# A mixture-of-experts forward pass: weights read in 32 KB runs per partition, with the contraction axes permuted to match

## The chip, the cores and the metric

The kernel runs on one NeuronCore of a Trainium2 chip. Five engines work side by side: TensorE (PE in the profile, its weight loads shown apart as PEld), VectorE (DVE), ScalarE (ACT), GpSimd (POOL) and SyncE (SP). Sixteen DMA engines move data between HBM and the on-chip SBUF; matmul results land in PSUM. The metric is the time of one execution in microseconds (us), lower is better.

## The reference

Eight experts, each with 256 tokens of width 512 and two weight matrices, all float32 in HBM:

```python
def reference(x, w1, w2):          # x (8,256,512)  w1 (8,512,2048)  w2 (8,2048,512)
    h = np.matmul(x, w1)
    h = np.maximum(h, 0)
    return np.matmul(h, w2).astype(np.float32)
```

One expert reads 4.19 MB of `w1`, 4.19 MB of `w2` and 0.52 MB of `x`, and writes 0.52 MB. No weight is used twice.

## The kernel before

All eight experts go through one loop. The DMA queue of GpSimd casts: it reads float32 weights and writes bf16 into SBUF, so 4.19 MB read become 2.10 MB written. `x` comes in as float32 through SP's queue.

**Layouts.** For a matmul, the axis that is summed over must lie on the 128 partitions. Before, partition `p` holds row `ko*128 + p` of a weight matrix for every block `ko`: four separate rows of `w1` (8 KB each in HBM) and sixteen separate rows of `w2` (2 KB each). The same holds for `x` and the output, with two rows of 2 KB per partition.

**One expert.** `x_sbuf` is transposed in eight 128x128 blocks in float32 (L65); each block goes to one PSUM tile and is copied, cast to bf16, by ScalarE (L68) before the next one may use that tile. The first layer (L79) is 64 matmuls: a 128x128 block of `w1` is the stationary operand and 256 columns of the transposed `x` stream past it. ScalarE applies the ReLU to pairs of results (L87). The second layer (L113) is 32 matmuls: a block of `hT` is stationary and 512 columns of `w2` stream. The loop over the two halves `mo` of the tokens is outside, the loop over the sixteen blocks `ko` inside. VectorE copies each half out of PSUM (L120) and SP stores both at once (L122).

**What sets the order.** Each engine runs its instructions in a fixed order that a scheduler wrote at build time; between engines there are semaphores. GpSimd issues the weight loads in the order w1, w2, w1, w2 (L71, L102), one queue, first in first out on each DMA engine. Both weight pools have four buffers, so the loads of four experts are queued at once and the load for expert e+4 is issued when expert e has been multiplied. The last expert's `w2` comes in four pieces of four blocks. The scheduler puts the last five transposes of an expert between its first matmuls of the first layer.

## Time and profile before

| what | value |
|---|---|
| median of three timed runs (lowest, highest) | 196.74 us (196.43, 199.07) |
| span of the profiled execution, first to last instruction | 196.1 us |
| its own time around the span | not listed; median minus span is 0.6 us |
| PE busy | 142.4 us, 73% |
| ACT busy, DVE busy, POOL busy | 55.4, 11.1, 17.8 us |
| weight queue (q0) as a share of 16 DMA engines | 93.7% |

The page's busy shares are averages over the whole span. For this kernel the DMA row of the 40 slices is the one to look at first: it reads 9 (90% or more) in all but the first and the last three slices, while the PE row changes between 5 and 9. "GB/s" counts what lands: for weights that is bf16, so the read side is twice that; `x` and the output count at their float32 size.

### The profile page before, as it was taken

Reading aid. Unit: us, or ns where it says so; the run is one execution under the profiler, and the core shown is the slowest. Engines: PE = TensorE matmul, PEld = TensorE weight load, DVE = VectorE, ACT = ScalarE, POOL = GpSimd, SP = SyncE. Lnnn points to the kernel's source line nnn. Section 1 sums busy time; section 2 is a strip of 40 time slices with the busy share of each in tenths; the row PEclk is TensorE's granted clock in tenths of the full one; section 3 lists DMA queues with packets and bytes.
Section 4 is the critical chain, followed back from the end, with each engine's and each line's share of the span. In section 5 each row is a group of like instructions: output and inputs, shape, how many; then the busy total and the mean of one; then the engine's idle time right before and its main releaser. Section 6 shows DMA issues by size and latency. Waiting matters only on the chain.

```text
span 196.1 us, 1934 instructions
## 1 busy us (share of the span) xinstructions
PE 142.4 (73%) x832; PEld 86.1 (44%) x832; DVE 11.1 (6%) x16; ACT 55.4 (28%) x129; POOL 17.8 (9%) x25
## 2 busy tenths in 40 slices
PE   0102899869398785959489696958997695959990
PEld 0001485348133572337334374425853482437740
DVE  0000000200011000200001100110002000200011
ACT  2100262137101470026300363022721271024500
POOL 8900001200102000020100100010001000010000
PEclk9999999999979999999958999995899999996999
DMA  5999999999999999999999999999999999999702
GB/s 206 226 236 203 200 232 242 208 243 252 225 216 205 250 255 218 214 221 249 244 216 208 208 259 253 216 206 253 212 218 208 248 212 219 215 216 237 121 0 107
DMA packets 25143, 42.05 MB, mean 214 GB/s; under 512 B 560, under 2 KB 16944, under 8 KB 25136
## 3 DMA queue, kind: packets, MB, share of 16 engines
q0 software_dynamic: 20784, 33.56, 93.7%
q1 hardware_dynamic: 4352, 8.39, 12.6%
q8 instruction: 6, 0.10, 0.2%
q14 instruction: 1, 0.01, 0.0%
HBM read 71.30 MB, written 4.19 MB: 385 GB/s over the span
## 4 chain that ended last, share of the span: by engine, by line
PE 58%; DMA 25%; another core or an unknown queue 7%; ACT 4%; POOL 2%; issue 2%; DVE 0%; POOLq 0%; ACTq 0%
PE o_psum L113 27%; DMA w_c<-in_w_dram 25%; PE h_psum L79 24%; PE xpsum L65 7%; ACT xT_sbuf L68 4%; POOL w_sbuf L71 1%; POOL w_c L102 1%; DVE out_sbuf L120 0%; POOL identity masks.py:199 0%; POOL identity masks.py:197 0%; POOLq masks.py:199 0%; ACTq L68 0%; POOLq L137 0%
## 5 line engine op out<-in xcount | busy, mean ns | idle before, releaser
L79 PE MATMUL h_psum<-xT_sbuf,w_sbuf 128*128 128x256 bf16 x512 | 67.3, 288 | 20.0 <-DMA w_sbuf<-in_w_dram 17.1
L113 PE MATMUL o_psum<-w_c,hT_sbuf 128*128 128x512 bf16 x256 | 61.3, 401 | 13.4 <-DMA w_c<-in_w_dram 13.4
L79 PEld LDWEIGHTS <-w_sbuf 128*128 128x128 bf16 x512 | 53.8, 106 | 30.5 <-DMA w_sbuf<-in_w_dram 18.4
L68 ACT CAST xT_sbuf<-xpsum 128x128 bf16<-128x128 f32 x64 | 17.0, 266 | 111.0 <-PE xpsum L65 111.0
L113 PEld LDWEIGHTS <-hT_sbuf 128*128 128x128 bf16 x256 | 25.9, 103 | 46.5 <-DMA w_c<-in_w_dram 11.1
L87 ACT ACTIVATE hT_sbuf<-h_psum 128x512 bf16<-128x512 f32 x64 | 37.1, 597 | 18.3 <-PE h_psum L79 18.1
L65 PE MATMUL xpsum<-identity,x_sbuf 128*128 128x128 f32 x64 | 22.0, 344 | 15.9 <-ACT xT_sbuf L68 11.3
L65 PEld LDWEIGHTS xpsum<-identity,x_sbuf 128*128 128x128 f32 x64 | 9.8, 153 | 28.0 <-ACT xT_sbuf L68 22.3
L120 DVE COPY out_sbuf<-o_psum 128x512 f32<-128x512 f32 x16 | 11.1, 692 | 181.4 <-PE o_psum L113 181.4
L102 POOL DMA_DIRECT2D w_c<-in_w_dram x11 | 11.2, 1014 | 100.2 <-PE xpsum L65 100.2
L71 POOL DMA_DIRECT2D w_sbuf<-in_w_dram x8 | 6.2, 779 | 53.6 <-PE h_psum L79 53.3
L68 ACT ACT_TABLE_LOAD x1 | 1.3, 1283 | 0.7 <-PEq L137 0.7
masks.py:199 POOL TENSOR_SCALAR_AFFINE_SELECT identity<-identity 128x128 f32<-128x128 f32 x1 | 0.3, 304 | 0.1
masks.py:197 POOL MEMSET identity<- 128x128 f32 x1 | 0.2, 204 | 0.3 <-POOLq L137 0.3
L137 POOL MEMSET const-float32-0.0<- 128x1 f32 x1 | 0.1, 98 | 0.2 <-issue 0.2
L137 POOL MEMSET const-bfloat16-1.0<- 128x1 bf16 x1 | 0.1, 101 | 0.0
L137 POOL MEMSET const-uint8-127<- 128x1 uint8 x1 | 0.1, 101 | 0.0
L137 POOL MEMSET const-float32-1.0<- 128x1 f32 x1 | 0.1, 98 | 0.0
## 6 DMA issues: line engine op xcount, KB each, us to landing
w_sbuf<-in_w_dram POOLq DMA_DIRECT2D x8, 2048.0 KB, 77.7
w_c<-in_w_dram POOLq DMA_DIRECT2D x7, 2048.0 KB, 80.7
x_sbuf<-in_x_dram SPq DMA_DIRECT2D x8, 512.0 KB, 7.7
out_dram<-out_sbuf SPq DMA_DIRECT2D x8, 512.0 KB, 6.9
w_c<-in_w_dram POOLq DMA_DIRECT2D x4, 512.0 KB, 42.1
```

The source lines that it names most:

```text
L65: nc.tensor.transpose(xpsum[:], x_sbuf[:, mo, ko * P:(ko + 1) * P], identity)
L68: nc.scalar.copy(xT_sbuf[:, ko, mo * P:(mo + 1) * P], xpsum[:])
L71: nc.gpsimd.dma_start(w1_sbuf[:], w1_tiled[e])
L79: nc.tensor.matmul(h_psum[:, mo_sub2 * capacity:(mo_sub2 + 1) * capacity], w1_sbuf[:, ko, mo * P:(mo + 1) * P], xT_sbuf[:, ko, :], start=( ...
L87: nc.scalar.activation(hT_sbuf[:, mo:mo + 2, :], h_psum[:], mybir.ActivationFunctionType.Relu,)
L102: nc.gpsimd.dma_start(w2_c[:], w2_tiled[e, :, ch * k2_chunk:(ch + 1) * k2_chunk, :])
L113: nc.tensor.matmul(o_psum[:], hT_sbuf[:, ko, mo * P:(mo + 1) * P], w2_sb[ch][:, ko_sub, :], start=(ko == 0), stop=(ko == K2 - 1),)
L120: nc.vector.tensor_copy(out_sbuf[:, mo, :], o_psum[:])
L137: nc = _bacc.Bacc("TRN2", target_bir_lowering=False, num_devices=1)
```

## The change

Which row of the summed axis lies on which partition is free, as long as both operands agree. The change numbers the rows the other way round: partition `p` takes consecutive rows. For `w1`, rows 4p to 4p+3, which is 32 KB in one piece in HBM; for `w2`, rows 16p to 16p+15, also 32 KB; for `x` and the output, rows 2p and 2p+1, 4 KB. With J = 16, hidden unit n = 16q+j must land on partition q of block j, so the stationary block of `w1` is now taken with a step of 16 columns, 32 bytes in bf16 (`w1_r[:, ko, b, :, j]`). `x` must be split as column 4q+ko: it is cast to bf16 on VectorE (`xb`), transposed in eight blocks with a step of four columns into one PSUM bank, and copied out by one VectorE instruction. The loads are issued one expert ahead of use in the program text, the depth of the weight pools stays four. The last expert's `w2` comes in pieces of 4, 4, 4, 2, 1 and 1 blocks in buffers of their own; its second layer loops over blocks outside and token halves inside, and its two halves are copied by VectorE and ScalarE and stored by SP and by ScalarE's queue.

```diff
-    x_tiled = x.rearrange("e (mo p) k -> e p mo k", p=P)
-    w1_tiled = w1.rearrange("e (ko p) n -> e p ko n", p=P)
-    w2_tiled = w2.rearrange("e (ko p) n -> e p ko n", p=P)
+    x_v = x.rearrange("e (p mo) k -> e p (mo k)", mo=MC)
+    out_v = out.rearrange("e (p mo) k -> e p (mo k)", mo=MC)
+    w1_v = w1.rearrange("e (p ko) n -> e p (ko n)", ko=K1)
+    w2_v = w2.rearrange("e (b p j) n -> e p b (j n)", p=P, j=J)
...
+            pieces = [4, 4, 4, 2, 1, 1]
+                c = w2_pool.tile([P, n * H], BF16, name=f"w2_last{i}", bufs=1)
+                nc.gpsimd.dma_start(c[:], w2_v[e, :, b, j * H:(j + n) * H])
...
-                nc.tensor.transpose(
-                    xpsum[:], x_sbuf[:, mo, ko * P:(ko + 1) * P], identity
-                )
-                nc.scalar.copy(xT_sbuf[:, ko, mo * P:(mo + 1) * P], xpsum[:])
+        nc.vector.tensor_copy(xb[:].rearrange("p m q k -> p (m q k)"), xs[e][:])
+        xt_ps = psum_t.tile([P, K1, MC, P], BF16, name="xt_ps")
+                nc.tensor.transpose(xt_ps[:, ko, mo, :], xb[:, mo, :, ko], identity[:])
+        nc.vector.tensor_copy(
+            xT[:].rearrange("p k c -> p (k c)"),
+            xt_ps[:].rearrange("p k m q -> p (k m q)"),
+        )
...
+        w1_r = w1s[e][:].rearrange("p (ko b q j) -> p ko b q j", ko=K1, b=NB, j=J)
-                        w1_sbuf[:, ko, mo * P:(mo + 1) * P],
+                        w1_r[:, ko, b, :, j],
...
+        if last:
+            order = [(k, m) for k in range(K2) for m in range(MC)]
+        else:
+            order = [(k, m) for m in range(MC) for k in range(K2)]
...
+                if last and m == 1:
+                    nc.scalar.copy(out_sb[:, m, :], o_ps[m][:])
+                else:
+                    nc.vector.tensor_copy(out_sb[:, m, :], o_ps[m][:])
+                if last:
+                    eng = nc.scalar if m == 1 else nc.sync
+                    eng.dma_start(out_v[e, :, m * H:(m + 1) * H], out_sb[:, m, :])
```

**Weight queue, GpSimd, end of the program.** Before (L71 loads `w1`, L102 `w2`; the shapes are partitions x rows x columns):

```order
L71 DMA w_sbuf<-in_w_dram 128x4x2048
L102 DMA w_c<-in_w_dram 128x16x512
L71 DMA w_sbuf<-in_w_dram 128x4x2048
L102 DMA w_c<-in_w_dram 128x4x512 x4
L148 UNCONDITIONAL_BRANCH
```

And of the change, the same place (L64 loads `w1`, L72 `w2`, L82 the last expert's pieces):

```order
L64 DMA w_sb<-in_w_dram 128x8192
L72 DMA w_sb<-in_w_dram 128x8192
L64 DMA w_sb<-in_w_dram 128x8192
L82 DMA w_last_932<-in_w_dram 128x2048
L82 DMA w_last_934<-in_w_dram 128x2048
L82 DMA w_last_936<-in_w_dram 128x2048
L82 DMA w_last_938<-in_w_dram 128x1024
L82 DMA w_last_940<-in_w_dram 128x512
L82 DMA w_last_942<-in_w_dram 128x512
```

The order of the loads is the same; each is now one run per partition, and the last `w2` is cut finer towards its end.

**TensorE, between the second layer of the seventh expert and the first layer of the eighth.** Before, from the transposes (L65) of the eighth expert on:

```order
L65 MATMUL xpsum_1143<-identity_58,x_sbuf_1140 128x128
L65 MATMUL xpsum_1146<-identity_58,x_sbuf_1140 128x128
L65 MATMUL xpsum_1149<-identity_58,x_sbuf_1140 128x128
L79 LDWEIGHTS w1_sbuf_1167
...
L65 MATMUL xpsum_1152<-identity_58,x_sbuf_1140 128x128
L65 MATMUL xpsum_1155<-identity_58,x_sbuf_1140 128x128
```

And of the change, the same place (L105 are the transposes, L119 the first layer, L140 the second):

```order
L140 MATMUL o_ps_1040<-w2_sb_793,hT_957 128x512
L105 LDWEIGHTS xb_1076
L105 MATMUL xt_ps_1078<-identity_88,xb_1076 128x128
...
L119 LDWEIGHTS w1_sb_929
L119 MATMUL h_ps_1090<-xT_1087,w1_sb_929 128x256
```

All eight transposes now stand ahead of the first layer, none between its matmuls.

**TensorE, the end of the last expert's second layer.** Before, where the first token half ends and the second begins (`o_psum_1259` and `o_psum_1277` are the halves, `w2_c_1250` the first piece of `w2`, `w2_c_1256` the last):

```order
L113 MATMUL o_psum_1259<-w2_c_1256,hT_sbuf_1169 128x512
L113 LDWEIGHTS hT_sbuf_1169
L113 MATMUL o_psum_1277<-w2_c_1250,hT_sbuf_1169 128x512
...
L113 MATMUL o_psum_1277<-w2_c_1256,hT_sbuf_1169 128x512
L148 UNCONDITIONAL_BRANCH
```

And of the change, the last rows (`o_ps_1171` and `o_ps_1172` are the halves):

```order
L140 MATMUL o_ps_1172<-w2_last3_938,hT_1089 128x512
L140 LDWEIGHTS hT_1089
L140 MATMUL o_ps_1171<-w2_last4_940,hT_1089 128x512
L140 LDWEIGHTS hT_1089
L140 MATMUL o_ps_1172<-w2_last4_940,hT_1089 128x512
L140 LDWEIGHTS hT_1089
L140 MATMUL o_ps_1171<-w2_last5_942,hT_1089 128x512
L140 LDWEIGHTS hT_1089
L140 MATMUL o_ps_1172<-w2_last5_942,hT_1089 128x512
```

Before, 20 of the 32 matmuls stand behind the first one that needs the last piece; now two matmuls need it, and they are the last ones.

## Rows read from the trace of the kernel before

**Rows 1.** DMA queues of the page: packets, MB landed, share of 16 engines.
```profile
q0 software_dynamic: 20784, 33.56, 93.7%
q1 hardware_dynamic: 4352, 8.39, 12.6%
```

**Rows 2.** Waits: engine, line, for whom; us in total, times, longest.
```profile
PE h_psum L79 <- DMA w_sbuf<-in_w_dram: 17.1, 6, 12.1
PE o_psum L113 <- DMA w_c<-in_w_dram: 13.4, 5, 3.4
```

**Rows 3.** Stretches with only w1 arriving: busy by engine, clock, DMA share, GB/s.
```profile
121.50:128.50 7.00, 7.00 (x33) 3.12 (x33) 0.69 (x1) 0.00 (x0) 0.00 (x0) 1.00 1.07 216
143.50:150.50 7.00, 6.73 (x32) 2.98 (x30) 1.03 (x2) 0.53 (x2) 0.08 (x1) 1.00 1.07 216
164.50:171.50 7.00, 6.86 (x33) 2.98 (x30) 0.90 (x2) 0.05 (x1) 0.00 (x0) 1.00 1.07 216
```

**Rows 4.** Same view, stretches with only w2 arriving.
```profile
108.50:112.50 4.00, 2.62 (x15) 1.32 (x13) 0.69 (x1) 1.55 (x6) 0.74 (x1) 1.00 1.24 208
158.00:162.00 4.00, 4.00 (x39) 3.52 (x36) 0.00 (x0) 3.12 (x6) 0.00 (x0) 1.00 1.24 208
180.00:183.00 3.00, 3.00 (x30) 2.69 (x29) 0.00 (x0) 2.45 (x5) 0.00 (x0) 1.00 1.25 207
```

**Rows 5.** Same view, the first two us, and where the load stream ends.
```profile
0.00:2.00 2.00, 0.00 (x0) 0.00 (x0) 0.00 (x0) 1.26 (x1) 1.14 (x6) 1.00 0.00 0
184.00:185.00 1.00, 1.00 (x10) 0.77 (x8) 0.00 (x0) 0.72 (x2) 0.00 (x0) 1.00 0.51 83
```

**Rows 6.** Timeline, PE and DVE in the tail: start, length, what [idle before].
```profile
164.17 7.08 PE L113 MATMUL o_psum<-w_c,hT_sbuf 128*128 128x512 bf16 x32 [1.98 <-DMA w_c<-in_w_dram]
173.90 0.61 PE L79 MATMUL h_psum<-xT_sbuf,w_sbuf 128*128 128x256 bf16 x4 [1.11 <-DMA w_sbuf<-in_w_dram]
178.24 6.56 PE L79 MATMUL h_psum<-xT_sbuf,w_sbuf 128*128 128x256 bf16 x52 [0.35 <-ACT xT_sbuf L68]
184.63 7.07 PE L113 MATMUL o_psum<-w_c,hT_sbuf 128*128 128x512 bf16 x32
191.74 0.69 DVE L120 COPY out_sbuf<-o_psum 128x512 f32<-128x512 f32 x1 [2.76 <-PE o_psum L113]
```

**Rows 7.** Chain of waits: start, length, what; first layer at full and at half clock.
```profile
156.35 5.84 PE h_psum L79 x52
175.30 0.44 PE h_psum L79 x4
176.82 0.85 PE h_psum L79 x4
```

**Rows 8.** Weight loads and transposes by line: ns min/median/max.
```profile
L79 PEld LDWEIGHTS <-w_sbuf x512: 95/98/208, 18.6 to 184.4; 128*128 128x128 bf16 x171
L113 PEld LDWEIGHTS <-hT_sbuf x256: 95/98/152, 30.5 to 191.1; 128*128 128x128 bf16 x128
L65 PEld LDWEIGHTS xpsum<-identity,x_sbuf x64: 137/138/231, 4.4 to 177.3; 128*128 128x128 f32 x64
L65 PE MATMUL xpsum<-identity,x_sbuf x64: 272/328/476, 4.4 to 177.5; 128*128 128x128 f32 x64
```

**Rows 9.** Timeline of GpSimd at the start: first weight load behind the identity's memset.
```profile
0.74 0.20 POOL masks.py:197 MEMSET identity<- 128x128 f32 x1 [0.29 <-POOLq L137]
1.27 0.87 POOL L71 DMA_DIRECT2D w_sbuf<-in_w_dram  x1 [0.33 <-issue]
```

**Rows 10.** Stretches around a fall of the PE clock (columns as in rows 3).
```profile
98.00:99.00 1.00, 0.39 (x1) 0.13 (x2) 0.00 (x0) 0.00 (x0) 0.00 (x0) 0.50 1.11 223
177.00:178.00 1.00, 0.89 (x5) 0.52 (x3) 0.00 (x0) 0.20 (x2) 0.00 (x0) 0.50 1.13 291
```

**Rows 11.** Timeline, PE: the first matmul in the first stretch of rows 10.
```profile
98.61 0.61 PE L113 MATMUL o_psum<-w_c,hT_sbuf 128*128 128x512 bf16 x1 [3.41 <-DMA w_c<-in_w_dram]
```

## The prediction

> **What bounds the kernel now.** I read the page's DMA queues first [rows 1]. The weight queue's packets fill 93.7% of sixteen engines. Its 20784 packets are 16384 rows of `w2` (2 KB read, 1 KB landed), 4096 rows of `w1` (8 KB read) and 16 for each of 19 loads: one packet for one run in HBM. Then the waits [rows 2]: TensorE waits for weights in both layers, 17.1 and 13.4 us, while the loads of four experts stand queued, so nothing holds the stream back. Then the busy time by stretches. Nothing lands in the first 2.0 us; in the second from 184 on 83 GB/s are left of some 208, so the stream ends at 184.4 [rows 4, 5]. Where only `w1` arrives, 216 GB/s land, 432 read [rows 3]; where only `w2` does, 208, or 416 read [rows 4]. At these rates a matrix (2.097 MB landed) takes 9.71 or 10.08 us, eight of each 158.3 us. Of the 182.4 us of stream 24.1 remain for eight `x` and seven outputs, 1.6 us each. Last the timeline of the tail [rows 6]: the eighth expert's first layer starts at 173.9, its second at 184.6, and the span ends at 196.1, 11.7 us after the stream. So the time is 2.0 of start, 182.4 of stream, 11.7 of tail.

> **The change, part by part.**

> *Longer runs.* One engine takes 2048 bytes at 416/16 = 26.0 GB/s in 78.8 ns, and 8192 at 27.0 in 303.4 ns [rows 3, 4]. The line through both is 3.9 ns a packet plus 27.4 GB/s. By it 32768 bytes take 1202 ns: 436 GB/s read, 218 landed, 9.62 us a matrix. That saves 0.46 us on each `w2`, 0.09 on each `w1`, 4.4 us over eight experts. `x` and the outputs go from 2 to 4 KB: 8 packets fewer per engine and transfer, 0.03 us, times 15 is 0.5 us. I take -4.9. Bounds: if long runs reach only the rate of 8 KB, `w2` alone gains 0.37 x 8 = 3.0; if they change nothing, 0. I take the line, since both of its points are the same queue in the same execution; that 32 KB lies fourfold beyond its last point stays in the range.

> *Start.* The first weight load is issued at 1.27, behind the identity's memset that started at 0.74 [rows 9]; now it stands first. Between 0 and -0.5; I take -0.4, as the queue's own start-up is the same.

> *Tail.* Let T be the end of the stream. Before, `w1` of the last expert was there 10.5 us ahead of T (173.9 to 184.4), 0.4 more than its `w2` alone takes, the share of an output stored meanwhile. Now 9.62 + 0.4: T-10.0. The first layer is 64 pairs of a weight load and a matmul; 52 took 5.84 us at full clock [rows 7], 112 ns each, so 7.2 us, no longer broken up by transposes: T-2.8. The second layer takes 7.08 us [rows 6]. It works through pieces as they land and only two matmuls need the last, so the weights do not hold it: T+4.3. A copy of 0.69 us, then the store: from the copy's end at 192.43 to the span's end 3.67 us [rows 6]. The two halves now go through two queues, but nearly together and with the same bytes, so I keep 3.67 (-0.5 is the other end). End: T+8.6 against T+11.7, -3.1 us.

> *TensorE in the steady state.* Per expert: first layer 7.2, second 7.08, eight transposes at between 0.098 (a hidden bf16 load) and 0.328 us (today's float32 matmul) [rows 8], 0.8 to 2.6, taken as 1.2 since they no longer wait for a copy each; then one copy of 1024 columns, nearest row 0.69 for 512 [rows 6], 0.7 to 1.4, taken as 1.2. Sum 16.7 us. The stream needs 2 x 9.62 + 1.57 for an output = 20.8. So 4.1 us are slack, and all of this costs nothing as long as a pair of the first layer stays under 112 + 4100/64 = 176 ns. If that cover goes, every ns above it costs 64 x 8 ns.

> *The step of 16 columns.* No row has a stationary load with a step. The contiguous ones take 98 ns at full clock and 152 at half [rows 8]: some 53 ns go with the clock, 45 do not, and all of it is hidden under the matmul, as the pair's 112 ns show. Bounds: hidden as now, 112 ns a pair; far end, the part that goes with the clock eightfold, some 430 ns. I take 112; a doubled part (151 ns, wholly exposed) would add 39 x 64 = 2.5 us, in the tail alone.

> [...]

> *Without cost.* VectorE gains eight casts and eight copies, at most 2.8 us per expert beside 1.4 of today, within 20.8. ScalarE loses its copies. SP's queue now holds six loads of `x` ahead of the first output. A packet of `x` then alternates with a weight packet of 1.2 us, eight times per engine, so `x` lands in about 10.8 us; it is issued an expert or more ahead, and the first one delays only the first layer's start, which no term of the sum holds. The last pieces of `w2` have buffers of their own, and wait only for loads that landed long before.

> **Sum.** -4.9 - 0.4 - 3.1 = -8.4 us on the profiled span of 196.1: 187.7. The median of the runs is 0.6 above that span, so **188.3 us**.

> **Rivals.**

> *TensorE becomes the bound (slower).* If the step makes a pair of the first layer take 213 ns, as at half clock (0.85 us for four [rows 7]), an expert needs 13.6 + 7.08 + 2.4 = 23.1 us, more than the stream's 20.8. First layer from about 14 us on, 8 x 20.7, 7 x 2.4 between, 4.4 at the end: 200.8, or 201.4 with the 0.6. It decides from 176 ns; at 430 ns it would be about 312 us. For it: every column lies in another place, and no row bears on that. Against it: the load may grow from 98 to 176 ns unseen. Chance 0.13.

> *Long runs bring nothing.* If both matrices go on at today's rates, or the sixteen engines, now walking runs that lie 128 KB apart, lose as much as the packets save, start and tail alone remain: -3.5, 193.2 us. For it: 2 to 8 KB brought only 4% [rows 3, 4]. Against it: 4% per packet is what is on offer, and `w1`, with the longer run, is the faster of the two. Chance 0.13. Should the queue cut the runs into 8 KB packets, so that the change does not do what it says, `w2` still gains 3.0 us: 190.2, inside the forecast's own range.

> *The clock.* TensorE's clock fell to half after a wait of 3.41 us [rows 10, 11], and again at 177, between waits for copies, costing the last first layer part of its speed. With slack of 4.1 us per expert it can fall again; only the last expert pays, 1.6 us for 3.4 us at half clock, 6.4 for a whole first layer. This is no case of its own but the upper part of the forecast.

> **How the numbers follow.** The forecast, stream still the bound and 186 to 192 us, has 0.74; the two rivals 0.13 each. The measurement tells 2% from no change, that is 192.8 and 200.7 us. So faster 0.74; within 2%, the second rival, 0.13; slower, the first, 0.13. The range takes in the forecast, its unknowns below (a line that runs on better, a quicker store) and the second rival: 185.3 to 196; outside it are the first rival and some 0.05 below.

> **What would show it.** Packets of the weight queue: 15 x 128 runs, 6 x 128 pieces and 21 x 16, or 3024. Landed rate 218 in both kinds of stretch; 208 would mean the second rival. Stream's end near 179. First-layer pairs at 112 ns and TensorE waiting for weights twice per expert; a weight load above 170 ns with TensorE never waiting would be the first rival. Behind the stream, the second layer's end 4.3 and the span's end 8.6 us later. The forecast is wrong if the stream's rate falls, or if TensorE's own 16.7 us become 20.8.

## The result and the profile after

The changed kernel takes **188.66 us** (median of four runs, 188.61 to 188.91) against 197.91 of the kernel before beside it (196.43 to 199.21): a ratio of 0.9545, 95% interval 0.9474 to 0.9617. Forecast were 188.3 us. The span of its profiled execution is 186.9 us, its own time 188.91, so 2.0 us lie around a span. I had put 0.6 there, the median before minus a span from another run; in the runs of the kernel before that stand beside the experiments it is some 1.8. On the spans alone the forecast was 187.7 and 186.9 came out: 9.2 us less instead of 8.4.

The DMA queues of the changed kernel (packets, MB landed, share of sixteen engines) answer to [rows 1]:

```profile
q0 software_dynamic: 3024, 33.56, 84.7%
q1 hardware_dynamic: 2304, 8.13, 11.5%
```

3024 packets, as worked out: every run of 32 KB is one packet. Its waits, which answer to [rows 2]:

```profile
PE h_ps L119 <- DMA w_sb<-in_w_dram: 28.3, 7, 10.6
PE o_ps L140 <- DMA w_sb<-in_w_dram: 17.2, 7, 3.7
```

TensorE still waits for weights in both layers, longer than before; the stream is still the bound. The end of the stream by seconds (busy time by engine, clock, DMA share, GB/s) answers to [rows 5]:

```profile
177.00:178.00 1.00, 1.00 (x6) 0.43 (x5) 0.00 (x0) 0.00 (x0) 0.00 (x0) 1.00 0.60 96
178.00:179.00 1.00, 1.00 (x6) 0.48 (x5) 0.00 (x0) 0.00 (x0) 0.00 (x0) 1.00 0.14 23
```

Read as before (23 of some 216 GB/s are left in the last second) it ends at 178.1, where it was 184.4: 6.3 us less. The rest of the span is 8.8 us, where it was 11.7: 2.9 us less. The two make up the 9.2. The last weight packet itself ends at 185.2 us in the trace before and at 178.5 in this one, which would make it 6.7 and 2.6: the division is good to half a us. The tail on TensorE and ScalarE, which answers to [rows 6], and the weight loads, which answer to [rows 8]:

```profile
157.82 8.75 PE L140 MATMUL o_ps<-w_sb,hT 128*128 128x512 bf16 x32 [3.69 <-DMA w_sb<-in_w_dram]
168.17 7.21 PE L119 MATMUL h_ps<-xT,w_sb 128*128 128x256 bf16 x64 [1.15 <-DMA w_sb<-in_w_dram]
175.21 7.07 PE L140 MATMUL o_ps<-w_last,hT 128*128 128x512 bf16 x32
182.32 0.59 ACT L149 COPY out_sb<-o_ps 128x512 f32<-128x512 f32 x1 [6.31 <-PE o_ps L140]
```
```profile
L119 PEld LDWEIGHTS <-w_sb x512: 142/144/178, 16.4 to 175.0; 128*128 128x128 bf16 x171
```

The last first layer is unbroken, 7.21 us instead of 10.7. A weight load of it takes 144 ns instead of 98, and 64 pairs still take 7.21 us, some 112 ns each as in [rows 7]: the longer load is hidden.

### The profile page after: what moved, and what is told of

It reads as the page before. It is cut to its first block, busy times and chain, and to the rows that moved or that the text cites. A ratio compares the mean times of both kernels' runs of the same rounds, so it can differ in the third digit from the quotient of the medians.

```text
span 186.9 us, 1894 instructions
## 1 busy us (share of the span) xinstructions
PE 131.1 (70%) x832; PEld 90.7 (49%) x832; DVE 20.2 (11%) x31; ACT 40.1 (21%) x66; POOL 12.4 (7%) x27
## 3 DMA queue, kind: packets, MB, share of 16 engines
q0 software_dynamic: 3024, 33.56, 84.7%
## 4 chain that ended last, share of the span: by engine, by line
PE 56%; DMA 25%; another core or an unknown queue 14%; POOL 1%; issue 1%; DVE 0%; ACT 0%; POOLq 0%; DVEq 0%
PE o_ps L140 30%; PE h_ps L119 25%; DMA w_sb<-in_w_dram 25%; PE xt_ps L105 1%; POOL w_sb L64 1%; DVE xT L107 0%; ACT out_sb L149 0%; POOL w_sb L72 0%; POOL identity masks.py:199 0%; POOL identity masks.py:197 0%; POOLq masks.py:199 0%; DVE out_sb L151 0%; DVEq L151 0%; DVEq L101 0%
## 5 line engine op out<-in xcount | busy, mean ns | idle before, releaser
L119 PE MATMUL h_ps<-xT,w_sb 128*128 128x256 bf16 x512 | 64.7, 293 | 29.2 <-DMA w_sb<-in_w_dram 28.3
L119 PEld LDWEIGHTS <-w_sb 128*128 128x128 bf16 x512 | 59.8, 147 | 33.6 <-DMA w_sb<-in_w_dram 29.5
L140 PE MATMUL o_ps<-w_sb,hT 128*128 128x512 bf16 x224 | 55.4, 410 | 17.2 <-DMA w_sb<-in_w_dram 17.2
L126 ACT ACTIVATE hT<-h_ps 128x512 bf16<-128x512 f32 x64 | 38.2, 597 | 135.8 <-PE h_ps L119 135.8
L140 PEld LDWEIGHTS <-hT 128*128 128x128 bf16 x256 | 26.4, 103 | 51.3 <-issue 26.5
L151 DVE COPY out_sb<-o_ps 128x512 f32<-128x512 f32 x15 | 10.4, 692 | 147.1 <-PE o_ps L140 147.1
L64 POOL DMA_DIRECT2D w_sb<-in_w_dram x8 | 4.9, 617 | 58.3 <-PE h_ps L119 57.6
L105 PE MATMUL xt_ps<-identity,xb 128*128 128x128 bf16 x64 | 5.3, 230 | 4.8 <-DVE xb L101 4.8
L105 PEld LDWEIGHTS <-xb 128*128 128x128 bf16 x64 | 4.7, 117 | 6.3 <-DVE xb L101 4.7
L101 DVE CAST xb<-x_sb 128x1024 bf16<-128x1024 f32 x8 | 5.5, 687 | 15.5 <-DMA x_sb<-in_x_dram 15.5
L140 PE MATMUL o_ps<-w_last,hT 128*128 128x512 bf16 x32 | 7.1, 379 | 0.0
L82 POOL DMA_DIRECT2D w_last<-in_w_dram x6 | 3.2, 530 | 51.5 <-DMA w_sb<-in_w_dram 51.5
L107 DVE COPY xT<-xt_ps 128x1024 bf16<-128x1024 bf16 x8 | 5.4, 681 | 0.0
L72 POOL DMA_DIRECT2D w_sb<-in_w_dram x7 | 3.7, 534 | 25.1 <-PE o_ps L140 25.1
```

The costliest lines, as they stand in the source:

```text
L64: nc.gpsimd.dma_start(t[:], w1_v[e])
L72: nc.gpsimd.dma_start(t[:], w2_v[e])
L82: nc.gpsimd.dma_start(c[:], w2_v[e, :, b, j * H:(j + n) * H])
L101: nc.vector.tensor_copy(xb[:].rearrange("p m q k -> p (m q k)"), xs[e][:])
L105: nc.tensor.transpose(xt_ps[:, ko, mo, :], xb[:, mo, :, ko], identity[:])
L107: nc.vector.tensor_copy(xT[:].rearrange("p k c -> p (k c)"), xt_ps[:].rearrange("p k m q -> p (k m q)"),)
```

## The experiments

All times are medians; every run lists a kernel before beside it, but that one wanders (196.4 to 200.6 us over all runs), so the small differences below are taken from the changed kernel's 188.66, whose own runs lie within 0.3 us. Runs of other versions lie up to 2 us apart (189.77 to 191.80 in experiment 4), so a difference below 1 us is a hint and no more.

**1. The tail of before.** One piece size, halves outside, both copies on VectorE and one store (the last two are not shown):

```diff
-            pieces = [4, 4, 4, 2, 1, 1]
+            pieces = [4, 4, 4, 4]
...
+        order = [(k, m) for m in range(MC) for k in range(K2)]
```

> The changed kernel (188.66 us) with the tail of before: the last w2 in four pieces of four, token halves outside, both copies on VectorE, one store. Theory A (the tail became shorter because the last first layer is no longer broken up by transposes): the first token half waits 0.3 us for the last piece and 20 matmuls follow it instead of 2, so the second layer ends 4.4 instead of 4.0 us after the stream: about 189.1. Rival B (the tail became shorter by the finer pieces and the exchanged loops): all 3.1 us come back, 191.8.

189.70 us, 1.0 more. TensorE in its tail:

```profile
168.09 7.21 PE L119 MATMUL h_ps<-xT,w_sb 128*128 128x256 bf16 x64 [1.38 <-DMA w_sb<-in_w_dram]
175.14 2.75 PE L137 MATMUL o_ps<-w_last,hT 128*128 128x512 bf16 x12
178.76 4.48 PE L137 MATMUL o_ps<-w_last,hT 128*128 128x512 bf16 x20 [0.87 <-DMA w_last<-in_w_dram]
```

Twelve matmuls, a wait of 0.87 us for the last piece, then twenty more. The second layer ends at 183.24 us instead of 182.28, which is the whole difference, so copies and store have no part in it. The finer pieces with the exchanged loops are worth 1 us, over twice the 0.4 that theory A gave them and a third of what rival B did.

**2. The new path of x alone**, in the kernel before:

```diff
+        nc.vector.tensor_copy(
+            xb[:].rearrange("p m k -> p (m k)"), x_sbuf[:].rearrange("p m k -> p (m k)")
+        )
+        xpsum = psum_t.tile([P, K1, M_CAP, P], bf16, name="xpsum")
...
-                xpsum = psum_t.tile([P, P], fp32, name="xpsum")
...
-                nc.scalar.copy(xT_sbuf[:, ko, mo * P:(mo + 1) * P], xpsum[:])
+        nc.vector.tensor_copy(
+            xT_sbuf[:].rearrange("p k c -> p (k c)"),
+            xpsum[:].rearrange("p k m q -> p (k m q)"),
+        )
```

`x` is cast to bf16 first, and one copy leaves PSUM behind eight transposes.

> The kernel before with one part of the change alone: x cast to bf16 on VectorE, eight transposes into one PSUM bank, one copy, all ahead of the first layer; all layouts, runs and the tail's loops as before. Theory A: the stream stays (ends near 184.4 us of the span) and the last first layer takes 7.2 instead of 10.7 us, so some 3.1 us less than the kernel before beside it. Rival B: no change (within 0.5 us).

196.0 us; ratio to the kernel before 0.9896, 0.9827 to 0.9966, so 2.1 us less, between 0.7 and 3.4. The stream stays where it was, and the last first layer is unbroken:

```profile
164.23 9.84 PE L121 MATMUL o_psum<-w_c,hT_sbuf 128*128 128x512 bf16 x32 [4.25 <-DMA w_c<-in_w_dram]
175.45 7.15 PE L87 MATMUL h_psum<-xT_sbuf,w_sbuf 128*128 128x256 bf16 x64 [0.94 <-DVE xT_sbuf L73]
182.43 2.75 PE L121 MATMUL o_psum<-w_c,hT_sbuf 128*128 128x512 bf16 x12
185.58 4.48 PE L121 MATMUL o_psum<-w_c,hT_sbuf 128*128 128x512 bf16 x20 [0.39 <-DMA w_c<-in_w_dram]
```

Its profile shows why it is not the whole 3.1: the last piece is waited for as in experiment 1, and twenty matmuls, 4.48 us, stand behind it from 185.58 on. The last first layer also began 1.5 us later than before, as the seventh expert's second layer ran partly at half clock (9.84 instead of 7.08 us; the clock row of its page reads 5 tenths in the slice from 165.3 to 170.2 us), but that only shortened the wait for the piece. Theory A holds for the larger part of the tail, rival B of experiment 1 for about 1 us of it.

**3 and 4. One matrix back in its old runs.** First J = 1, which also takes the step out of `w1`'s blocks, then `w1` by `(ko p)` with `x` split to match:

```diff
-J = 16
+J = 1
...
```
```diff
-    w1_v = w1.rearrange("e (p ko) n -> e p (ko n)", ko=K1)
+    w1_v = w1.rearrange("e (ko p) n -> e p ko n", ko=K1)
...
```

> The changed kernel with J = 1: w2 again in runs of 2 KB (sixteen rows 128 apart), stationary blocks of w1 without a step; w1, x and the output in the new layout. Theory A (3.9 ns a packet of w2 is what the stream gained): 8 x 0.46 = 3.7 us more, 192.4; weight loads back at 98 ns. Rival C (the stream gained by the rows of x and of the output, or by loads issued earlier): 188.7.

> The changed kernel with w1 in four runs of 8 KB as before (x split to match), everything else as changed. Theory A: 8 x 0.09 = 0.7 us more, 189.4. Rival C: 188.7. If the stream's gain is larger than the line through 2 and 8 KB says because 32 KB runs are better still: 2 us more, 190.7.

192.52 and 189.94 us: 3.9 and 1.3 more. Rival C alone is out: the weights' runs do matter. But the two do not fit the line: `w1` counts almost twice what it should.

**5. No step in the stationary blocks:**

```diff
-                        w1_r[:, ko, b, :, j],
+                        w1s[e][:, ko * F + (pr * 2 + s) * P:ko * F + (pr * 2 + s + 1) * P],
```

> The changed kernel with contiguous stationary blocks of w1 (128 neighbouring columns instead of every sixteenth), all loads and everything else as changed; the hidden units are then paired with the wrong rows of w2, so the output is another one. Theory A (the step makes a weight load 46 ns longer, all of it hidden under the matmul): loads 98 ns instead of 144, time unchanged, 188.7. Rival D (a part of it shows, in the last first layer at least): 64 x 0.046 = 2.9 us less, 185.8.

188.61 us against 188.66, the same. The loads are back at 98 ns:

```profile
L117 PEld LDWEIGHTS <-w_sb x512: 96/98/151, 16.4 to 174.4; 128*128 128x128 bf16 x171
```

The step of 16 columns costs 46 ns a load and nothing in time. Theory A, not D.

**6. `w2` in runs of 8 KB:**

```diff
-J = 16
+J = 4
```

> The changed kernel with J = 4: w2 in runs of 8 KB, stationary blocks with a step of 4 columns (8 bytes). Theory A by the line of 3.9 ns a packet: 8 x 0.09 = 0.7 us more than the changed kernel, 189.4; weight loads of 113 ns as the transposes' (their step is also 8 bytes). If longer runs go on helping beyond the line: up to 190.7. If 32 KB packets hinder x and the outputs: less than 188.7.

189.41 us, 0.75 more, and loads of 113 ns: both as expected of the line. That the time fitted was chance, as experiment 8 shows.

**7. The load by its step**, with 128 moving columns:

```diff
+                    mov = xT[:, ko, :P]
+                    if pr == 0:
+                        w = w1s[e][:, base:base + 128:1]
+                        nc.tensor.matmul(out_h, w, mov, start=(ko == 0), stop=(ko == K1 - 1))
...
+                    elif pr == 7:
+                        w = w1s[e][:, base:base + 8129:64]
...
```

> The changed kernel with 128 instead of 256 moving columns (half of the tokens are left out) and stationary blocks of w1 with steps of 1, 2, 4, 5, 8, 16, 32 and 64 columns, one step for each pair of blocks and each on its own line (other columns than the right ones). Measures the weight load by its step where the matmul no longer hides it. [...] Rival (the load grows on with the step): clearly over 144 at 32 and 64.

A single execution. Nanoseconds min/median/max of a load with a step of 1, 4, 8, 16, 32 and 64 columns (2 and 5 columns: 98 and 118), and the timeline of groups of eight pairs, steps 1 and 2 and then 16 and 32:

```profile
L122 PEld LDWEIGHTS <-w_sb x64: 95/98/151, 16.4 to 169.0; 128*128 128x128 bf16 x64
L128 PEld LDWEIGHTS <-w_sb x64: 112/113/151, 18.0 to 169.9; 128*128 128x128 bf16 x64
L134 PEld LDWEIGHTS <-w_sb x64: 142/146/155, 19.9 to 170.9; 128*128 128x128 bf16 x64
L137 PEld LDWEIGHTS <-w_sb x64: 146/148/155, 20.4 to 171.4; 128*128 128x128 bf16 x64
L140 PEld LDWEIGHTS <-w_sb x64: 141/150/162, 20.9 to 171.9; 128*128 128x128 bf16 x64
L143 PEld LDWEIGHTS <-w_sb x64: 171/204/219, 21.4 to 172.5; 128*128 128x128 bf16 x64
```
```profile
148.05 0.61 PE L122 MATMUL h_ps<-xT,w_sb 128*128 128x128 bf16 x8 [0.93 <-DVE xT L107]
148.50 0.61 PE L125 MATMUL h_ps<-xT,w_sb 128*128 128x128 bf16 x8
150.33 0.66 PE L137 MATMUL h_ps<-xT,w_sb 128*128 128x128 bf16 x8
150.83 0.66 PE L140 MATMUL h_ps<-xT,w_sb 128*128 128x128 bf16 x8
```

From one group's start to the next it is 0.45 us at step 1 (56 ns a pair) and 0.50 at step 16 (62 ns), while a load alone takes 98 and 148 ns. So the longer load is pipelined, too. From 8 to 32 columns the load grows by no more than 4 ns (146 to 150); at 64 (128 bytes) the rival's growth sets in, 204 ns, and there eight pairs take 0.74 us (from 171.98 to the next matmul at 172.72), 92 ns each. The load jumps to 146 ns at a step of 16 bytes, but 113 and 118 ns at 8 and 10 bytes lie before it; at 256 moving columns the step of 32 bytes shows nowhere in the time (experiment 5).

**8. Weights alone.** Two loads of `x`, one output:

```diff
-            load_x(e + 2)
+            xs[e + 2] = xs[e % 2]
...
-        if not last:
-            nc.sync.dma_start(out_v[e], out_sb[:].rearrange("p m h -> p (m h)"))
```

> The changed kernel with only two loads of x (used in turn) and only the last output stored; the other seven outputs are left out. The stream is then weights in 32 KB runs alone. Theory A (9.62 us a matrix by the line through 2 and 8 KB): 16 x 9.62 = 153.9 us plus 2.5 for two x, stream's end at 158.2. If 32 KB runs are better than the line: at 435 GB/s read and more the end comes below 157; if x and the outputs had cost less than 1.5 us each, above 159.

A single execution. Read as before, the stream ends at 160.4, the last of the cases expected. Two waits for `w2`, five experts apart (timeline):

```profile
44.87 7.07 PE L140 MATMUL o_ps<-w_sb,hT 128*128 128x512 bf16 x31 [2.47 <-DMA w_sb<-in_w_dram]
142.08 8.75 PE L140 MATMUL o_ps<-w_sb,hT 128*128 128x512 bf16 x31 [2.23 <-DMA w_sb<-in_w_dram]
```

97.21 us for ten matrices: 9.72 us each, 216 GB/s landed, just what `w1` had in its runs of 8 KB [rows 3]. The line through 2 and 8 KB does not go on: **32 KB are no faster than 8 KB.** So `w2` gained 10.08 - 9.72 = 0.36 us an expert, 2.9 us in all, and `w1` nothing. The stream's 176.2 us (178.1 less 1.9 of start) hold 155.5 of weights and 20.7 for the fifteen transfers of `x` and outputs, 1.4 us each instead of 1.6: 3.4 us came from there.

**9 and 10. Where the small transfers gained.** `x` and output back in rows of 2 KB beside long weight runs, then the reverse (experiments 3 and 4 together):

```diff
-    x_v = x.rearrange("e (p mo) k -> e p (mo k)", mo=MC)
-    out_v = out.rearrange("e (p mo) k -> e p (mo k)", mo=MC)
+    x_v = x.rearrange("e (mo p) k -> e p mo k", mo=MC)
+    out_v = out.rearrange("e (mo p) k -> e p mo k", mo=MC)
...
```

> The changed kernel with x and the output in two rows of 2 KB per partition as before, weights in 32 KB runs. Weights alone now take 9.72 us a matrix, no less than w1 took before, so 3.1 us of the stream's 5.95 us must have come from the 15 transfers of x and outputs (1.6 us each before, 1.4 now). Theory F (from their own longer rows): all of it comes back, 191.8. Theory G (from the longer weight packets that they alternate with): nothing comes back, 188.7.

> The changed kernel with both weights in the runs of before (w1 8 KB, w2 2 KB), x and the output in 4 KB rows, the new tail. w2 alone costs 8 x 0.36 = 2.9 us more. Theory F (x and outputs gained by their own rows): 188.7 + 2.9 = 191.6. Theory G (they gained by the length of the weight packets beside them): 3.1 more, 194.7.

The first takes **210.63 us**, 6.3% more than the kernel before (1.0627, 1.0562 to 1.0693), and neither theory had that. VectorE's timeline shows it, with the wait ahead of each cast of an `x` and, from 106 on, of copies that need a stored output's buffer:

```profile
26.89 0.69 DVE L101 CAST xb<-x_sb 128x1024 bf16<-128x1024 f32 x1 [19.98 <-DMA x_sb<-in_x_dram]
47.22 0.69 DVE L101 CAST xb<-x_sb 128x1024 bf16<-128x1024 f32 x1 [11.82 <-DMA x_sb<-in_x_dram]
66.86 0.69 DVE L101 CAST xb<-x_sb 128x1024 bf16<-128x1024 f32 x1 [10.00 <-DMA x_sb<-in_x_dram]
86.41 0.69 DVE L101 CAST xb<-x_sb 128x1024 bf16<-128x1024 f32 x1 [8.65 <-DMA x_sb<-in_x_dram]
106.03 1.29 DVE L151 COPY out_sb<-o_ps 128x512 f32<-128x512 f32 x2 [18.93 <-DMA out_dram<-out_sb]
125.56 0.69 DVE L101 CAST xb<-x_sb 128x1024 bf16<-128x1024 f32 x1 [17.65 <-DMA x_sb<-in_x_dram]
145.19 1.29 DVE L151 COPY out_sb<-o_ps 128x512 f32<-128x512 f32 x2 [18.94 <-DMA out_dram<-out_sb]
```

One transfer of SP's queue lands about every 19.6 us. It has 16 packets of 2 KB on each DMA engine, and a 32 KB weight packet takes 9.72/8 = 1.215 us: 16 x 1.215 = 19.4. By these figures, 19.6 us against 19.4, each small packet waits for one weight packet. An expert needs two such transfers, 39 us, while its weights take 19.4; `x` and the outputs become the bound, and TensorE waits for `x` instead. The weights themselves are not late: the second row has 2 GB/s landing from 180 to 190 us, of a span of 208.5:

```profile
PE h_ps L119 <- DVE xT L107: 42.8, 4, 22.6
```
```profile
180.00:190.00 10.00, 9.01 (x55) 5.22 (x55) 1.98 (x3) 1.70 (x3) 0.00 (x0) 1.00 0.01 2
```

With rows of 4 KB a transfer has 8 packets on each engine, so the two of an expert have 16, as many as its two matrices. By 8 x 1.215 they would take 9.7 us each, but the changed kernel has no such room to spare. In its trace nine transfers of SP's queue land one right behind the other from 16.1 to 105.1 us, 11.1 us apart (the prediction had 10.8), 22.3 an expert. The first layers, which wait for weights, start 22.1 us apart in that stretch (39.21 to 105.44, three experts) and 20.9 behind it (105.44 to 168.17); the last row is SP's longest wait for an `x`, 11.1 us:

```profile
39.21 8.88 PE L119 MATMUL h_ps<-xT,w_sb 128*128 128x256 bf16 x64 [4.24 <-DMA w_sb<-in_w_dram]
105.44 7.21 PE L119 MATMUL h_ps<-xT,w_sb 128*128 128x256 bf16 x64 [1.97 <-DMA w_sb<-in_w_dram]
```
```profile
SPq L59 <- DMA x_sb<-in_x_dram: 13.2, 3, 11.1
```

Between 16.1 and 105.1 us, 1024 packets of 4 KB and 1030 of 32 KB start in the changed kernel's trace: the two queues keep pace one for one, and it is still weights that TensorE waits for. The transfers of both versions show it in their time to landing (DMA issues: count, KB each, median us), the changed kernel first, then experiment 9:

```profile
x_sb<-in_x_dram SPq DMA_DIRECT2D x8, 512.0 KB, 27.9
out_dram<-out_sb SPq DMA_DIRECT2D x7, 512.0 KB, 15.1
```
```profile
x_sb<-in_x_dram SPq DMA_DIRECT2D x8, 512.0 KB, 50.4
out_dram<-out_sb SPq DMA_DIRECT2D x7, 512.0 KB, 67.6
```

The reverse takes 192.83 us, 4.2 more, between theory F (2.9) and theory G (6.0). Its stream ends at 182.3, 180.4 us long; less 158.3 for weights at the old rates, 22.1 remain, 1.5 us a transfer. Of the 3.4 us that the small transfers gained, then, 2.0 came with their own rows (24.1 to 22.1) and 1.4 with the longer weight packets beside them (22.1 to 20.7). By the last weight packets (185.2, 183.2 and 178.5 us) the two shares are 1.8 and 1.9, so they are known to half a us. The second share is also what must stand behind the 1.3 us of experiment 4 and the 0.75 of experiment 6, where the weights' own rate stayed, and behind 1.0 of the 3.9 in experiment 3. Experiments 3 and 4 together make more of it (2.3) than experiment 10 (1.4), so what each matrix adds stays open. Why a small transfer is cheaper beside long packets no run shows.

**11 and 12. A version that beats both.** In the tail of the changed kernel 32 matmuls, 7.07 us, begin 2.9 us ahead of the stream's end. If both last first layers are computed ahead of both last second layers, TensorE can follow the pieces:

```diff
...
+            load_w1(e + 1)
+            load_w1(e + 2)
+            load_w2(e + 1)
+            load_w2(e + 2)
...
+    stage2(E - 2)
+    stage2(E - 1)
```

> A version meant to beat both: the last four matrices are loaded in the order w1 of expert 7, w1 of 8, w2 of 7, w2 of 8, both w2 in pieces of 4, 4, 4, 2, 1, 1 blocks, both first layers computed ahead of both second layers, so that TensorE keeps up with the pieces and only two matmuls are left when the stream ends (w2 pool of three buffers, PSUM banks 3 and 4 instead of 4 and 3). In the changed kernel 4.0 us of matmuls and 0.6 of a copy lie behind the stream's end, then 4.0 to the end. Theory A: the second layer ends 0.5 us after the stream instead of 4.0, so 3.5 us less than the changed kernel: 185.1. Rival: TensorE's clock falls between the pieces and it lags, or the stream runs dry behind the pieces' waits: 187 or more.

186.94 us (ratio to the kernel before 0.9434, 0.9379 to 0.9489), between theory and rival. The profiled run shows the rival's clock: a stretch of the last first layer, and that layer with the wait ahead of it:

```profile
157.00:158.00 1.00, 0.53 (x3) 0.46 (x4) 0.00 (x0) 0.00 (x0) 0.29 (x1) 0.50 1.06 225
```
```profile
157.47 9.98 PE L118 MATMUL h_ps<-xT,w_sb 128*128 128x256 bf16 x64 [3.42 <-DMA w_sb<-in_w_dram]
167.29 13.98 PE L142 MATMUL o_ps<-w_last,hT 128*128 128x512 bf16 x62
```

Granted clock 0.50, 9.98 us instead of 7.2, and the matmuls end at 181.3, 4.0 us behind the last weight packet (177.3). So the wait was filled with 48 transposes that nobody reads:

```diff
+        if e == E - 1:
+            keep_busy(e, 6)
         stage1(e)
```

> The version with the last four matrices reordered (e8_last_two, 186.94), and in the wait between the first layers of the last two experts 48 transposes whose result nobody reads (some 2.7 us of TensorE). In e8_last_two's profile the clock was at half from 156.7 to 163.3, behind that wait of 3.42 us: the last first layer took 9.98 instead of 7.2 us and the matmuls ended 3.1 us after the stream. Theory A: with the wait filled the clock stays at full, the matmuls end 0.5 us after the stream, 185.1. Rival (the lag is not the clock's): 186.9 as before, or more by the time that the extra work delays the first layer.

**186.33 us** (0.9395, 0.9335 to 0.9455), 2.3 less than the changed kernel, the lowest of all:

```profile
154.82 2.84 PE L99 MATMUL xt_ps<-identity,xb 128*128 128x128 bf16 x48
158.38 7.22 PE L126 MATMUL h_ps<-xT,w_sb 128*128 128x256 bf16 x64 [0.72 <-DMA w_sb<-in_w_dram]
165.44 13.72 PE L150 MATMUL o_ps<-w_last,hT 128*128 128x512 bf16 x62
179.80 0.59 PE L150 MATMUL o_ps<-w_last,hT 128*128 128x512 bf16 x2 [0.64 <-DMA w_last<-in_w_dram]
```
```profile
158.00:159.00 1.00, 0.62 (x6) 0.62 (x7) 0.00 (x0) 0.00 (x0) 0.38 (x1) 1.00 1.07 221
```

The clock holds (1.00 granted, the last row) and TensorE now waits for the very last piece: the matmuls end at 180.4, 0.9 us behind the last weight packet (179.5) instead of 4.0. That much is nearly as theory A had it. But this stream ends 2.2 us later than in experiment 11, which has the same loads in the same pieces and order, and 1.0 later than in the changed kernel; so neither the pieces nor their issue can be all of the 1.2 us that are missing of the 3.5 expected, and what moved the end stays open. In time the filled wait gained 0.6 us over experiment 11, whose runs overlap with these (186.32 to 188.03 against 186.19 to 186.96): that gain is not clear of the noise, and the last layer's clock in experiment 11 is known for the profiled run alone.

## Why the prediction was right, point by point

The number and the mechanism were right, the division of the gain was not, and that the number came out so close was luck.

*What bounds it: right.* Both kernels wait for the stream; the packets are 3024 as worked out.

*Longer runs: the sum too small, its terms mis-sized.* The term was -4.9 us; the stream became 6.2 us shorter (182.4 to 176.2). `w2` was put at -3.7 and gained 2.9, `w1` at -0.7 and gained nothing (experiment 8): the rate of 432 GB/s read is already reached at 8 KB, and "I take the line" was the failing choice; the bound named beside it, 3.0, was the truth. `x` and the outputs were put at -0.5 and gave -3.4, from their rows and from the packets beside them (experiments 9 and 10), of which the per-packet time of 3.9 ns knew nothing.

*Start: wrong.* The first weight load is issued at 1.23, not 0.74; it no longer waits for the memset, but nothing else could go out earlier. The start, 2.0 by the rows, is 1.9: some 0.1 us. What lands first is `x`, which I took for the weights. The first weight packet starts at 4.5 us instead of 5.0, near the 0.4 of the forecast, but not for its reason; which one it is no run shows.

*Tail: right in size, a little wrong in cause.* -3.1 forecast, -2.9 measured (2.6 by the last packets). The unbroken first layer carries the larger part (experiment 2), but the pieces and loops, which the walk counted as a mere condition, 1 us of it (experiment 1).

*TensorE's slack and the step: right.* Pairs at 112 ns, loads from 98 to 144 ns, no time (experiment 5). The 20.8 us that I set against TensorE's 16.7 hold an output but leave out the load of `x`; the first layers start 21.5 us apart (39.21 to 168.17, six experts), so the slack was larger than I gave it. The first rival was farther off than I gave it: even at 128 moving columns a step of 16 makes a pair only 6 ns longer (56 to 62). What the step costs a load was my estimate: the 144 ns lie near the 151 of the doubled part, and no run shows the eightfold one behind the 430 ns a pair.

*The second rival* had its price from the wrong place. What could have undone the change were not sixteen engines in HBM, which landed 216 GB/s in 32 KB runs (experiment 8), but the small queue behind the long packets; how far apart the runs of one engine lie no run shows. The prediction worked that out, a packet of `x` behind each weight packet, eight times, and filed it under "without cost". With 16 packets instead of 8 it costs 22 us (experiment 9); the outputs take their turn there as well, which I had not added.

*The final number* came out within 0.4 us by luck, because two errors met: the span fell by 0.8 us more than forecast in the profiled run and by 1.0 in the median one, and 1.4 us more than I had put lie around it.

## What to carry to other kernels

Before lengthening the runs of one queue, count the packets that the other queues need per round, times the duration of one long packet, and set that against the period of the stream. Here 32 small packets an expert, 39 us by that count beside 19.4 of weights, made the kernel 6.3% slower than the one before (experiment 9); 16 of them, 19.4 by the count and 22.3 measured beside first layers 22.1 us apart, left it at 0.9545 of the time before. Halving the small queue's packet count decided the sign of the whole change. A rate per run length is to be extended only as far as its rows reach: here, in the weights' own rate, 2 to 8 KB brought 4%, 8 to 32 KB nothing. Runs of 8 KB in both matrices with the 4 KB rows of `x` were not tried. A step of 16 columns in the stationary operand cost no time beside 256 moving columns (experiment 5) and 6 ns a pair beside 128 (experiment 7); there a layout may be chosen for the DMA's sake.
